# The first feed-forward of a two-block layer stack by seven block products

## The chip, the cores and the metric

The kernel runs on one core of one Trainium2 chip. The time is the device time of one execution in microseconds (us); the median of several executions is what a version is judged by. The engines are named as in the profile: PE is TensorE's matmul, PEld its weight load, DVE VectorE, ACT ScalarE, POOL GpSimd, SP SyncE, which issues most of the loads.

## The reference, cut to the stage that changes

Two blocks work on 1024 tokens (1040 rows with 16 meta rows in front) of width 1024. The first block ends in a gated feed-forward of width 2816, which is 22 tiles of 128:

```python
D_FF, CONV_WIDTH, N_META = 2816, 3, 16

def causal_dwconv(x, w, b):
    L = x.shape[1]
    xp = jnp.pad(x, ((0, 0), (CONV_WIDTH - 1, 0), (0, 0)))
    y = b
    for j in range(CONV_WIDTH):
        y = y + xp[:, j:j + L] * w[j]
    return y

...
        h = h + rmsnorm(z @ w_out[l], mix_norm_post[l])
        u = rmsnorm(h, ffn_norm_pre[l])
        gt = causal_dwconv(u @ ffn_w_gate[l], ffn_conv_w[l], ffn_conv_b[l])
        y = (jax.nn.gelu(gt, approximate=True) * (u @ ffn_w_up[l])) @ ffn_w_down[l]
        h = h + rmsnorm(y, ffn_norm_post[l])
    return h[:, N_META:]
```

The second block follows: attention and an mLSTM side by side, a cross-attention over 256 memory rows, and 32 experts. It starts with a norm of h and a projection.

## The kernel before, in words

Everything is kept feature by token: 128 features on the partitions, tokens along the free axis. Fp32 accuracy comes from splitting both operands of every matmul into a high part (an fp32r copy, made by ACT) and a low part (the rest, a subtraction on DVE). `mm3` (lines 417 to 424) then does three matmuls for each k tile: high by high, high by low, low by high. SBUF is an arena of 48 slots of 1040 fp32 columns (`Slots`), taken and given back by hand. `Stream` (line 194) loads weight blocks of 128x1024 in the fixed order that `all_blocks` lists, and splits them ahead of their use (lines 228 and 229).

PSUM has eight banks in three rings: four `mm`, two `lv`, two `ms`. Work that should run later is put off with `K.after(us, fn)`; `K.tick` counts matmul columns as a clock and calls what is due (lines 394 to 402). Step-wise background work hangs in `K.bg` and moves one step for each tile (`K.step`). After the program is written, a scheduler sets the order in which each engine's instructions stand; each engine then takes them strictly in that order.

`ffn` (line 1099) does the feed-forward of the first block. `gu` (line 1124) makes the gate of an f tile in three chunks of 342 tokens (the first three f tiles together in chunks of 256 or 258, as their input comes out of the preceding stage in these chunks), then `gate_conv` the convolution on DVE and the gelu on ACT, then the up product in two chunks of 512, whose result `up_out` multiplies with the gelu and splits into m's parts. `down` (line 1138) takes two f tiles of m and adds their part of all eight output tiles to y in SBUF: 16 results of 512 tokens, each 6 matmuls and one DVE addition (line 1149). So for each two f tiles PE does 144 matmuls of 342 columns and 192 of 512.

The last `down` goes token chunk by token chunk (256), and `last` hangs a `post_pre` (line 554) behind each of the four chunks. `post_pre` is the seam between two stages: `first` (norm of the result, residual, squares) and, later, `second` (the next stage's norm and the split of its input by `norm_apply`, line 579). DVE, ACT and POOL share this work. While it runs, `mem_kv` (line 1587) gives PE the keys and values of the memory rows, and `block2_mix` (line 1206) starts with `tm`, eight token tiles of 24 matmuls of 392 columns that read the normed tokens.

Of the kernel before, what the change touches and what calls it, by code (L numbers as in the profile page):

```python
# [20 lines left out]
D = 1024  # L21
KT = 8
# [171 lines left out]
class Stream:  # L194


    def __init__(self, k, blocks, raw=3, ahead=2):
        self.k, self.blocks = k, blocks
        self.raw_n, self.ahead = raw, ahead
        self.loaded = self.split = self.taken = 0  # L200
        self.raw, self.parts = {}, {}
        self.rings, self.own = {}, ()

# [16 lines left out]
    def pump(self):  # L220
        k = self.k
        while self.split < min(self.taken + self.ahead, len(self.blocks)):
# [13 lines left out]
    def _load(self):  # L236
        k = self.k
        while self.loaded < len(self.blocks) and len(self.raw) < self.raw_n:
# [64 lines left out]
class Kern:  # L303
# [250 lines left out]
    def post_pre(self, s, n, yv, hv, post, pre, store, uh, ul, t1=2.0, t2=18.0, done=None):  # L554
# [14 lines left out]
        def second():  # L569
# [5 lines left out]
            self.norm_apply(yv, hv, r, pre, uh, ul, n)  # L575
# [26 lines left out]
def block1(K):  # L602
# [458 lines left out]
    def ev_y(f, ps, s, n):  # L1061
        nc.scalar.activation(K.f(y + f, s, s + n), ps[:, :n], AF.Copy)
        K.sum_sq(s, n, ps[:, :n], f == 0)
        if f < 7:
# [5 lines left out]
                   done=lambda: c < 2 and hload(c + 2))  # L1070
# [18 lines left out]
MEMF = 18  # L1089
LAG, HS, GS = 3, 4, 3  # L1090
DEC = {256: ((0, 4),)}
# [6 lines left out]

def ffn(K, u2h, u2l, h1d, rest, y):
    nc, sl, st = K.nc, K.sl, K.st  # L1100
    act = K.act([u2h + k for k in range(8)], [u2l + k for k in range(8)])
    ms = {}

    def gate_conv(f, g):
# [10 lines left out]
    def up_out(f, c, ps, s, n):  # L1115
        x = s - 16
        nc.vector.tensor_mul(K.f(c, x, x + n), ps[:, :n], K.f(c, x, x + n))
        if f not in ms:
            ms[f] = sl.take()
        nc.scalar.activation(K.r(ms[f], x, x + n), K.f(c, x, x + n), AF.Copy)  # L1120
        nc.vector.tensor_sub(K.r(c, x, x + n), K.f(c, x, x + n), K.rf(ms[f], x, x + n))

    def gu(fs):
# [5 lines left out]
        K.dense((len(fs),), 8, Q1026 if fs[0] == 0 else C1026, act, ev_g)  # L1129
        if fs[0] == 0:  # L1130
            rest()
        cs = [gate_conv(f, g) for f, g in zip(fs, gs)]
        K.dense((len(fs),), 8, C1024, act, lambda j, ps, s, n: up_out(fs[j], cs[j], ps, s, n))
        for f, c in zip(fs, cs):
            ms[f] = (ms[f], c)

    def down(g, last=None):
        ks = [2 * g, 2 * g + 1]
        ws = [st.next() for _ in ks]
        order = [(o, c) for c in QX for o in range(8)] if last else [(o, c) for o in range(8) for c in CX]  # L1140
        for o, (s, n) in order:
            ps = K.bank("dn")[:, :n]
            wh = [K.r(w[0], o * 128, o * 128 + 128) for w in ws]
            wl = [K.r(w[1], o * 128, o * 128 + 128) for w in ws]
            K.mm3(ps, wh, wl, [K.r(ms[k][0], s, s + n) for k in ks], [K.r(ms[k][1], s, s + n) for k in ks])
            if g == 0:
                nc.scalar.activation(K.f(y + o, s, s + n), ps, AF.Copy)
            else:
                nc.vector.tensor_add(K.f(y + o, s, s + n), ps, K.f(y + o, s, s + n))  # L1149
            if last:  # L1150
                last(o, s, n)
            K.tick(3 * len(ks), n)
        for w in ws:
            st.done(w)
        for k in ks:
            sl.give(ms[k][0])
            sl.give(ms[k][1])

    st.ahead = 2
    gu([0, 1, 2])  # L1160
    for f in range(3, NF + 1):
        if f == MEMF:
            mt = sl.take(2)
            mem = mem_norm(K, mt)
            sl.give(mt, 2)
        if f % 2 == 1:
            down((f - 3) // 2)
        if f < NF:
            gu([f])

    uh, ul = u2h, u2l
    st.ahead = 1
    xd = K.dram.tile([128, 8, T2], F32, name="xd")
    K.sums(QX)
    hcs = [sl.take(2) for _ in range(2)]
# [5 lines left out]
    def last(o, s, n):  # L1181
        K.sum_sq(s, n, K.f(y + o, s, s + n), o == 0)
        if o < 7:
            return
        c = QX.index((s, n))
        K.post_pre(s, n, K.f3(y, 8, s, n), K.flat3(hcs[c % 2], KT, n), "ffn_post", "norm_mix",
                   xd[:, :, s:s + n], K.r3(uh, 8, s, n), K.r3(ul, 8, s, n),
                   t1=2.5 + 8.0 * c, t2=20.0 + 8.0 * c, done=lambda: c < 2 and hload(c + 2))

    hload(0)  # L1190
    hload(1)
    down(NF // 2 - 1, last)

    def rest():
# [5 lines left out]
        st.ahead = 2  # L1200

# [4 lines left out]
def block2_mix(K, uh, ul, xd, rest):  # L1206
# [7 lines left out]
    def tm(nb, kb, n, evac):  # L1214

        ws = [st.next() for _ in range(nb)]
        for t in range(8):
# [29 lines left out]
    tm(4, 2, 392, ev_c)  # L1247
    rest()
# [232 lines left out]
    for h in range(4):  # L1481
# [4 lines left out]
        if h == 3:  # L1486

            atl = sl.take(4)
            av = K.f3(atl, 4, 0, T2)
            nc.sync.dma_start(av, attd.rearrange("j p t -> p j t"))  # L1490
            for k in range(4):
                nc.vector.scalar_tensor_tensor(av[:, k], av[:, k], K.p("att_out", k), K.f(asq, 0, T2), op0=OP.mult, op1=OP.mult)
# [94 lines left out]
def mem_kv(K, mh, ml):  # L1587
# [3 lines left out]
    kx, vx = sl.take(), sl.take()  # L1591
# [591 lines left out]
def all_blocks(A):  # L2183
    b = [A["w1"][j] for j in range(A["w1"].shape[0])]
    G, U, W = A["w_gate"], A["w_up"], A["w_down"]
    b += [G[0], G[1], G[2], U[0], U[1], U[2]]
    for f in range(3, NF + 1):
        if f % 2 == 1:
            b += [W[f - 3], W[f - 2]]
        if f < NF:  # L2190
            b += [G[f], U[f]]
    b += [W[NF - 2], W[NF - 1]]
# [10 lines left out]
    return b  # L2203


def program(ctx, tc, A, out, dbg=None):
    K = Kern(ctx, tc, A, out, dbg)
    K.load_consts()
    K.st = Stream(K, all_blocks(A))
# [43 lines left out]
```

## Time and profile before

| | us |
|---|---|
| median of 3 runs (2885.87 to 2891.96) | 2886.0 |
| the profiled execution | 2889.72 |
| its span, first to last instruction | 2887.9 |
| PE busy | 2739.0 |
| DVE busy | 1735.2 |
| ACT busy | 1357.0 |
| POOL busy | 451.3 |
| first feed-forward, first gate result to last down result | 765.5 to 1519.4 |

A busy PE is not a PE at its peak, since matmuls overlap in the records: the time of a matmul in a stream is read from the distance between results, not from its own duration. Where times of a row are spaced more closely than its duration, the spacing is what a further instruction costs.

### The profile page before, as it was taken

Reading aid. Unit: us, or ns where it says so; the run is one execution under the profiler, and the core shown is the slowest. Engines: PE = TensorE matmul, PEld = TensorE weight load, DVE = VectorE, ACT = ScalarE, POOL = GpSimd, SP = SyncE. Lnnn points to the kernel's source line nnn. Section 1 sums busy time; section 2 is a strip of 40 time slices with the busy share of each in tenths; the row PEclk is TensorE's granted clock in tenths of the full one; section 3 lists DMA queues with packets and bytes.
Section 4 is the critical chain, followed back from the end, with each engine's and each line's share of the span. In section 5 each row is a group of like instructions: output and inputs, shape, how many; then the busy total and the mean of one; then the engine's idle time right before and its main releaser. Section 6 shows DMA issues by size and latency. Waiting matters only on the chain. (4 is left out here: it accounts for less than half of the span.)

```text
span 2887.9 us, 40429 instructions
## 1 busy us (share of the span) xinstructions
PE 2739.0 (95%) x15834; PEld 2346.6 (81%) x15834; DVE 1735.2 (60%) x2658; ACT 1357.0 (47%) x2267; POOL 451.3 (16%) x452
## 2 busy tenths in 40 slices
PE   7999999999899999999998999999998999899995
PEld 7999999999888888888887877778897666666663
DVE  7755621144734444445459264785746899999985
ACT  5546432234431221223135265553544788687775
POOL 4322120034500000000035000011401111111110
PEclk8999999999999999999999999999999999999997
DMA  4000113333511111111115111022116999999996
GB/s 156 23 30 23 37 66 110 115 122 86 117 59 52 44 50 46 52 44 39 64 59 161 66 45 52 15 98 86 34 69 224 333 358 364 327 356 369 365 361 225
DMA packets 118944, 382.74 MB, mean 133 GB/s; under 512 B 13100, under 2 KB 29612, under 8 KB 117984
## 3 DMA queue, kind: packets, MB, share of 16 engines
q1 hardware_dynamic: 88080, 319.71, 30.5%
q0 software_dynamic: 11040, 38.56, 5.3%
q10 hardware_dynamic: 19632, 21.87, 2.7%
q8 instruction: 125, 2.05, 0.3%
q14 instruction: 67, 0.55, 0.1%
HBM read 338.12 MB, written 46.16 MB: 133 GB/s over the span
## 5 line engine op out<-in xcount | busy, mean ns | idle before, releaser
L422 PE MATMUL ps_mm<-r,r 128*128 128x342 f32 (+6 forms) x2928 | 967.3, 330 | 4.2 <-DVE f L1037 2.3
L424 PE MATMUL ps_mm<-r,r 128*128 128x342 f32 (+6 forms) x2928 | 957.1, 327 | 1.9 <-DVE r L229 1.9
L423 PE MATMUL ps_mm<-r,r 128*128 128x342 f32 (+6 forms) x2928 | 954.1, 326 | 0.0
L229 DVE TENSOR_TENSOR r<-f,r 128x1024 fp32r<-128x1024 f32 (+1 forms) x549 | 659.7, 1224 | 443.3 <-ACT r L228 270.2
L228 ACT ACTIVATE r<-f 128x1024 fp32r<-128x1024 f32 (+1 forms) x549 | 569.7, 1056 | 477.8 <-PE ps_lv L423 156.0
L422 PEld LDWEIGHTS ps_mm<-r,r 128*128 128x128 f32 x2928 | 554.0, 189 | 40.6 <-issue 7.9
L424 PEld LDWEIGHTS ps_mm<-r,r 128*128 128x128 f32 x2928 | 553.5, 189 | 30.6 <-DVE r L229 3.0
L423 PEld LDWEIGHTS ps_mm<-r,r 128*128 128x128 f32 x2928 | 554.4, 189 | 28.9 <-DVE r L1500 0.3
L2055 PE MATMUL ps_mm<-r,r 128*96 128x512 f32 x512 | 207.2, 405 | 31.2 <-DVE r L229 31.2
L2054 PE MATMUL ps_mm<-r,r 128*96 128x512 f32 x512 | 204.8, 400 | 0.6 <-ACT r L228 0.6
L2056 PE MATMUL ps_mm<-r,r 128*96 128x512 f32 x512 | 202.3, 395 | 0.0
L1149 DVE TENSOR_TENSOR f<-ps_lv,f 128x512 f32<-128x512 f32 (+1 forms) x176 | 112.4, 642 | 103.9 <-PE ps_lv L424 103.6
L422 PE MATMUL ps_lv<-r,r 128*128 128x512 f32 (+1 forms) x384 | 146.7, 382 | 7.1 <-DVE f L1149 7.1
L423 PE MATMUL ps_lv<-r,r 128*128 128x512 f32 (+1 forms) x384 | 145.6, 379 | 0.0
L424 PE MATMUL ps_lv<-r,r 128*128 128x512 f32 (+1 forms) x384 | 144.9, 377 | 0.0
L2055 PEld LDWEIGHTS ps_mm<-r,r 128*96 128x96 f32 x512 | 83.1, 162 | 70.6 <-DVE r L229 41.5
L694 ACT ACTIVATE f<-ps_mm 128x342 f32<-128x342 f32 (+2 forms) x99 | 44.8, 454 | 162.9 <-PE ps_mm L424 162.7
L2054 PEld LDWEIGHTS ps_mm<-r,r 128*96 128x96 f32 x512 | 83.1, 162 | 39.5 <-ACT r L228 7.6
L2030 POOL DMA_INDIRECT f<-xnd,lix x32 | 51.6, 1612 | 368.6 <-PE ps_lv L2056 303.2
L2056 PEld LDWEIGHTS ps_mm<-r,r 128*96 128x96 f32 x512 | 83.0, 162 | 31.1
L2054 PE MATMUL ps_lv<-r,r 128*96 128x512 f32 x256 | 102.2, 399 | 0.6 <-ACT r L2084 0.6
L2055 PE MATMUL ps_lv<-r,r 128*96 128x512 f32 x256 | 101.7, 397 | 0.0
(466 smaller groups left out, 3934.2 us busy)
## 6 DMA issues: line engine op xcount, KB each, us to landing
f<-in_e_gate_dram SPq DMA_DIRECT2D x128, 512.0 KB, 9.8
f<-in_e_down_dram SPq DMA_DIRECT2D x128, 512.0 KB, 9.9
f<-in_e_up_dram SPq DMA_DIRECT2D x128, 512.0 KB, 8.5
f<-in_w_dram SPq DMA_DIRECT2D x52, 512.0 KB, 4.0
f<-in_w_gate_dram SPq DMA_DIRECT2D x22, 512.0 KB, 3.6
f<-in_w_up_dram SPq DMA_DIRECT2D x22, 512.0 KB, 3.2
f<-in_w_down_dram SPq DMA_DIRECT2D x22, 512.0 KB, 3.3
gates<-f ACTq DMA_DIRECT2D x16, 513.0 KB, 6.1
```

Source lines behind the costliest of these rows:

```text
L228: k.nc.scalar.activation(k.r(h, 0, n), k.f(r, 0, n), AF.Copy)
L229: k.nc.vector.tensor_sub(k.r(l, 0, n), k.f(r, 0, n), k.rf(h, 0, n))
L422: mm(ps, wh[k], ah[k], start=start and k == 0, stop=False)
L423: mm(ps, wh[k], al[k], start=False, stop=False)
L424: mm(ps, wl[k], ah[k], start=False, stop=stop and k == n - 1)
L694: nc.scalar.activation(K.f(slot, s, s + n), ps[:, :n], AF.Copy)
L1149: nc.vector.tensor_add(K.f(y + o, s, s + n), ps, K.f(y + o, s, s + n))
L2030: nc.gpsimd.indirect_dma_start(out=K.f(g, 0, D)[:EB], out_offset=None, in_=R["xnd"][:, :], in_offset=IndirectOffsetOnAxis(ap=ix[:, 0:1], a ...
L2054: mm(ps, xh, wh, start=first, stop=False)
L2055: mm(ps, xh, wl, start=False, stop=False)
L2056: mm(ps, xl, wh, start=False, stop=last)
```

## The change

The 22 f tiles are 11 pairs. Two pairs (f 0 to 3) are still done as before, without `down`. For the other nine pairs, gate and up are each a product of a 2x2 block matrix of weights (two f tiles by two halves of k) with a 2x2 block matrix of inputs (two halves of k by two halves of tokens, 514 each with two columns of overlap). It is done as seven products of blocks in place of eight: the class `Seven` makes four sums of weight blocks and the splits, `u_sums` and `u_parts` make the four sums of input blocks once, and `seven` does the seven products, each of 12 matmuls of 258 or 256 columns, in two chunks, with five additions on DVE behind them. Gate and up of a pair are called a pass each.

`down` is done at the end for all 22 f tiles: seven products, named 11, s1, s2, s3, s4, 12 and 22 by the weight block or sum that they use, of 11 steps each (one for each pair). A step is 12 matmuls of 512 columns into four banks. `keep` forms three sums of m's quarters and stores four quarters and three sums unsplit to DRAM (`mo`); a step loads one of them (256 KB) and a piece of the weights (256 or 512 KB), and `split` makes the parts. `result` adds the products into the quarters of y. The `post_pre` of tokens 512 to 1023 (chunks 2 and 3) is due during 12 and 22, that of chunks 0 and 1 behind 22. The norm of the memory rows moves from the middle of the feed-forward to behind s4. `tm` starts with token tiles 4 to 7, and finishes the put-off work before tile 0. At the seam ahead of the feed-forward, `first` is due at 4.5 in place of 2.0, and `norm_apply` leaves POOL out there (`n_pool=0`), as the input sums need y complete. Behind it the attention's output is loaded and split slot by slot.

```diff
+class Seven:
...
+        V.tensor_sub(s3, a11, a21)
+        V.tensor_add(s1, a21, a22)
+        yield
+        V.tensor_sub(s2, s1, a11)
+        V.tensor_sub(s4, a12, s2)
+        yield
+        high(ha, a)
+        yield
+        high(hb, b, 512, 528)
+        low(ha, a)
...
+HC = ((0, 258), (258, 256))
+WAIT = 5
...
+    def keep(j, cs, t):
...
+        V.tensor_sub(t1, m12, m11)
+        V.tensor_sub(m12, m22, m12)
+        V.tensor_sub(t2, m22, t1)
+        V.tensor_sub(t4, t2, m21)
+
+        def store():
+            for src, o, n in ((cs[0], 0, 2), (cs[1], 2, 2), (t[0], 4, 2), (t[1], 6, 1)):
+                nc.scalar.dma_start(mo[j, :, o:o + n], K.f(src, 0, 512 * n).rearrange("p (o n) -> p o n", o=n))
...
+        K.after(KEEP, store)
...
+    def seven(w, c0, n, at, first):
+
+        r12, r21, r22 = at
+        A_, D_, F_, E_, G_ = K.bank(), K.bank("lv"), K.bank(), K.bank("ms"), K.bank("lv")
+        product(A_, n, w.side("11"), "11", c0, True, True)
+        nc.scalar.activation(r12, A_[:, :n], AF.Copy)
+        product(D_, n, w.side("s3"), "t3", c0, True, True)
+        product(E_, n, w.side("s1"), "t1", c0, True, True)
+        nc.scalar.activation(r22, E_[:, :n], AF.Copy)
+        product(F_, n, w.side("22"), "t4", c0, True, True)
+        product(A_, n, w.side("12"), "21", c0, False, True)
+        first(A_)
+        product(G_, n, w.side("s2"), "t2", c0, True, True)
+        V.tensor_add(r12, G_[:, :n], r12)
+        V.tensor_add(r21, D_[:, :n], r12)
+        product(E_, n, w.side("s4"), "22", c0, False, True)
+        V.tensor_add(r22, r22, r21)
+        V.tensor_sub(r21, r21, F_[:, :n])
+        V.tensor_add(r12, E_[:, :n], r12)
...
+    def pair(j, wg):
...
+        wu = Seven(K, A["w_up"][fs[0]], A["w_up"][fs[1]])
+        group(wg, wu, gate)
+        wg.give()
+        cs = [gate_conv(f, g) for f, g in zip(fs, gs)]
...
+            V.tensor_mul(cc, r21[:, d:n], cc)
+            V.tensor_mul(ce, r22, ce)
+            V.tensor_mul(cb, r12, cb)
...
+        group(wu, wg, up)
...
+        keep(j, cs, t)
...
+    order = (("11", "11"), ("s1", "t1"), ("s2", "t2"), ("s3", "t3"), ("s4", "22"), ("12", "21"), ("22", "t4"))
...
+    gu([0, 1], mid0)
+    gu([2, 3], mid1)
+    K.drain()
...
+    for _ in u_parts("t1", [(u2h + k, HT[1]) for k in range(4)], q11, y, HT[0]):
+        pass
+    for _ in u_parts("t2", [(u2l + k, HT[1]) for k in range(4)], q22, y + 4, HT[1]):
+        pass
...
+        elif w == "s4":
+            squares(1, y12, False)
+            post((2, 3), 8.0, 22.0, 9.0)
...
+            mem.extend(mem_norm(K))
...
+        elif w == "22":
+            squares(0, y21, False)
+            post((0, 1), 6.0, 20.0, 7.0)
+
+    tags = {"11": "mm mm mm mm", "s1": "lv lv ms ms", "s2": "mm mm mm mm", "s3": "lv lv ms ms", "s4": "mm mm mm mm",
+            "12": "lv lv mm mm", "22": "mm mm lv lv"}
+    for i, (w, m, j) in enumerate(steps):
+        while len(loads) < min(i + LOADS - (w in ("12", "22")), len(steps)):
+            load()
+        while len(sides) < min(i + SIDES, len(steps)):
+            split()
+        if j == 0:
+            banks = [K.bank(t) for t in tags[w].split()]
+        a, b = sides[i]
+        mh, ml = K.r(b, 512, 1024), K.r(b, 0, 512)
+        for o in range(4):
+            wh, wl = K.r(a, 512 + o * 128, 640 + o * 128), K.r(a, o * 128, o * 128 + 128)
+            mm = nc.tensor.matmul
+            mm(banks[o], wh, mh, start=j == 0, stop=False)
+            mm(banks[o], wh, ml, start=False, stop=False)
+            mm(banks[o], wl, mh, start=False, stop=j == NP - 1)
...
-    tm(4, 2, 392, ev_c)
-    rest()
+    tm(4, 2, 392, ev_c, rest)
```

The order on DVE in the feed-forward before, one f tile (L229 is the low part of a weight block, L1108 and L1110 the convolution, L1117 and L1121 the product with the gelu and its split, L1149 the 16 additions into y):

```order
L229 TENSOR_TENSOR r_1_3351<-f_1_148,r_1_2061 128x1024
L1108 TENSOR_SCALAR f_1_433<-f_1_379,prm 128x1024
L1110 SCALAR_TENSOR_TENSOR f_1_433<-f_1_379,prm,f_1_433 128x1024 x2
L1117 TENSOR_TENSOR f_1_433<-ps_mm,f_1_433 128x512
L1121 TENSOR_TENSOR r_1_3343<-f_1_433,r_1_1603 128x512
L1117 TENSOR_TENSOR f_1_433<-ps_mm,f_1_433 128x512
L229 TENSOR_TENSOR r_1_193<-f_1_136,r_1_191 128x1024
L1121 TENSOR_TENSOR r_1_3343<-f_1_433,r_1_1603 128x512
L1149 TENSOR_TENSOR f_8_5488<-ps_lv,f_8_5488 128x512 x16
```

And now on DVE in the first chunk of a pair's up pass (L1187 ends the convolution of the two gates, L1140 to L1144 are the sums of the next pair's gate weights, L1138 a low part, L1287 to L1292 the additions behind the products, L1321 to L1324 the products with the gelu):

```order
L1187 SCALAR_TENSOR_TENSOR f_1_160<-f_1_352,prm,f_1_160 128x1024
L1321 TENSOR_TENSOR f_1_74<-ps_mm,f_1_74 128x254
L1140 TENSOR_TENSOR f_1_143<-f_1_120,f_1_136 128x512
L1143 TENSOR_TENSOR f_1_137<-f_1_137,f_1_120 128x512
L1287 TENSOR_TENSOR f_1_142<-ps_lv,f_1_142 128x258
L1144 TENSOR_TENSOR f_1_143<-f_1_120,f_1_137 128x512
L1288 TENSOR_TENSOR f_1_142<-ps_lv,f_1_142 128x258
L1138 TENSOR_TENSOR r_1_343<-f_1_120,r_1_199 128x1024
L1290 TENSOR_TENSOR f_1_148<-f_1_148,f_1_142 128x258
L1292 TENSOR_TENSOR f_1_142<-ps_ms,f_1_142 128x258
L1291 TENSOR_TENSOR f_1_142<-f_1_142,ps_mm 128x258
```

The additions behind the products now stand behind the two convolutions and between the sums and splits of the next weights.

DVE at the end of the down products, from the second norm of chunk 2 on (L576 and L1927 are reciprocals of norms, L593 to L598 `norm_apply`, L1376 the split of a step, L1469 the four additions that free the banks of product 12):

```order
L576 RECIPROCAL f_1_74<-f_1_74 128x256
L1376 TENSOR_TENSOR r_1_348<-f_1_154,r_1_348 128x512
L593 SCALAR_TENSOR_TENSOR f_8_5488<-f_2_12089,prm,f_1_74 128x256 x5
L1376 TENSOR_TENSOR r_1_2061<-f_1_124,r_1_2061 128x512
L595 TENSOR_TENSOR r_8_164<-f_8_5488,r_8_163 128x2x256 x2
L595 TENSOR_TENSOR r_8_164<-f_8_5488,r_8_163 128x256
L598 SCALAR_TENSOR_TENSOR r_8_164<-f_8_5488,prm,r_8_163 128x256 x3
L1927 RECIPROCAL f_1_149<-f_1_149 128x256
L1469 TENSOR_TENSOR f_8_5488<-ps_lv,f_8_5488 128x512
L593 SCALAR_TENSOR_TENSOR f_2_5456<-f_2_5456,prm,f_1_149 128x256 x5
```

The remaining three L1469 stand behind the memory rows' `norm_apply`; before the change, no norm stood between the additions of `down` and PE's next matmul into their banks except in the last `down`.

## Rows read from the trace of the kernel before

**Rows 1.** The page: busy time, share of the span and instructions by engine.

```profile
PE 2739.0 (95%) x15834; PEld 2346.6 (81%) x15834; DVE 1735.2 (60%) x2658; ACT 1357.0 (47%) x2267; POOL 451.3 (16%) x452
```

**Rows 2.** Stretches: length, busy PE, PEld, DVE, ACT, POOL, granted clock, DMA share, GB/s.

```profile
1002.04:1069.46 67.42, 67.42 (x337) 58.78 (x336) 30.00 (x38) 13.32 (x18) 0.00 (x0) 1.00 0.14 48
660.00:680.00 20.00, 20.00 (x170) 20.00 (x169) 2.45 (x2) 7.69 (x17) 4.10 (x5) 1.00 0.37 132
1484.00:1602.00 118.00, 99.60 (x560) 90.29 (x560) 100.46 (x165) 64.25 (x130) 61.95 (x75) 0.91 0.40 131
2500.00:2600.00 100.00, 95.93 (x481) 67.48 (x479) 92.12 (x116) 79.76 (x96) 14.76 (x10) 1.00 1.02 360
```

**Rows 3.** Timeline of ACT, copies behind 24 matmuls: start, duration, then what.

```profile
1014.87 0.46 ACT L1127 ACTIVATE f<-ps_mm 128x342 f32<-128x342 f32 x1 [2.44 <-PE ps_mm L424]
1018.65 0.46 ACT L1127 ACTIVATE f<-ps_mm 128x342 f32<-128x342 f32 x1 [3.32 <-PE ps_mm L424]
...
660.93 0.38 ACT L1062 ACTIVATE f<-ps_mm 128x256 f32<-128x256 f32 x1 [2.17 <-PE ps_mm L424]
663.77 0.39 ACT L1062 ACTIVATE f<-ps_mm 128x256 f32<-128x256 f32 x1 [2.18 <-PE ps_mm L424]
...
680.93 0.39 ACT L1062 ACTIVATE f<-ps_mm 128x258 f32<-128x258 f32 x1 [2.20 <-PE ps_mm L424]
683.83 0.39 ACT L1062 ACTIVATE f<-ps_mm 128x258 f32<-128x258 f32 x1 [2.23 <-PE ps_mm L424]
```

**Rows 4.** Timeline of DVE: results of `down`, then dense runs (xN in one row).

```profile
1045.59 0.69 DVE L1149 TENSOR_TENSOR f<-ps_lv,f 128x512 f32<-128x512 f32 x1 [0.72 <-PE ps_lv L424]
1046.99 0.69 DVE L1149 TENSOR_TENSOR f<-ps_lv,f 128x512 f32<-128x512 f32 x1 [0.71 <-PE ps_lv L424]
...
1036.13 1.28 DVE L1149 TENSOR_TENSOR f<-ps_lv,f 128x512 f32<-128x512 f32 x2
...
1504.35 0.74 DVE L1149 TENSOR_TENSOR f<-ps_lv,f 128x256 f32<-128x256 f32 x2
...
1024.50 0.81 DVE L1108 TENSOR_SCALAR f<-f,prm 128x1024 f32<-128x1024 f32 x1
1025.34 2.60 DVE L1110 SCALAR_TENSOR_TENSOR f<-f,prm,f 128x1024 f32<-128x1024 f32 x2
```

**Rows 5.** Groups of instructions: the weight loads of line 422, busy us, mean ns.

```profile
L422 PEld LDWEIGHTS ps_mm<-r,r 128*128 128x128 f32 x2928 | 554.0, 189 | 40.6 <-issue 7.9
```

**Rows 6.** DMA: issues with us to landing; queues with packets, MB, share.

```profile
f<-in_w_down_dram SPq DMA_DIRECT2D x22, 512.0 KB, 3.3
...
q1 hardware_dynamic: 88080, 319.71, 30.5%
...
q10 hardware_dynamic: 19632, 21.87, 2.7%
```

**Rows 7.** PE's waits from 640 to 765 (us, times, longest), and DVE at chunk 3.

```profile
PE ps_ms L546 <- POOL f L540: 10.5, 4, 7.4
...
783.93 3.25 DVE L591 SCALAR_TENSOR_TENSOR f<-f,prm,f 128x256 f32<-128x256 f32 x5
```

**Rows 8.** Timeline of DVE: parts of `post_pre` at the end of the feed-forward.

```profile
1494.62 1.74 DVE L548 RECIPROCAL f<-f 128x256 f32<-128x256 f32 x1
...
1496.56 1.75 DVE L562 SCALAR_TENSOR_TENSOR f<-f,prm,f 128x256 f32<-128x256 f32 x2
...
1533.86 3.49 DVE L591 SCALAR_TENSOR_TENSOR f<-f,prm,f 128x256 f32<-128x256 f32 x5
...
1540.00 2.35 DVE L229 TENSOR_TENSOR r<-f,r 128x1024 fp32r<-128x1024 f32 x2
```

**Rows 9.** Groups by shape: one operation of DVE beside busy POOL, and without.

```profile
L562 DVE SCALAR_TENSOR_TENSOR f<-f,prm,f 128x256 f32<-128x256 f32 x56 | 44.1, 826 | 0.0
...
L596 DVE SCALAR_TENSOR_TENSOR r<-f,prm,r 128x256 fp32r<-128x256 f32 x36 | 15.7, 475 | 0.1
```

More of the change, by code (lines that the diff above doesn't have):

```diff
@@ L1 @@
 import math
+from functools import partial
 from contextlib import ExitStack
@@ L221, in pump @@
         k = self.k
-        while self.split < min(self.taken + self.ahead, len(self.blocks)):
+        while self.split < min(self.taken + self.ahead, self.limit):
             self._load()
@@ L1069, in ev_y @@
                    h1d[:, :, s - T0:s - T0 + n], K.r3(u2h, 8, s, n), K.r3(u2l, 8, s, n),
-                   done=lambda: c < 2 and hload(c + 2))
+                   t1=4.5, done=lambda: c < 2 and hload(c + 2), n_pool=0)
     hload(0)
@@ L1159, in ffn, with up_out, act0 @@
[L1159 to L1169, printed above, removed]
+        def up_out(j, ps, s, n):
+            c = K.f(cs[j], s - 16, s - 16 + n)
+            V.tensor_mul(c, ps[:, :n], c)
+        def act0(s, n):
+            if s == Q1026[-1][0]:
+                rest()
+            return act(s, n)
@@ new lines, in early, with product @@
+    def early():
+        for _ in u_sums():
+            yield
+        for n, q, lo, l0 in (("t3", q12, HT[1], y), ("t4", q21, HT[0], y + 4)):
+            t = [sl.take() for _ in range(2)]
+            new.extend(t)
+            yield from u_parts(n, [(t[k // 2], k % 2 * HN) for k in range(4)], q, l0, lo)
+    def product(ps, n, w, b, c0, start, stop):
+        wh, wl = w
+        bh, bl = ops[b]
+        K.mm3(ps[:, :n], wh, wl, [K.r(x, o + c0, o + c0 + n) for x, o in bh], [K.r(x, o + c0, o + c0 + n) for x, o in bl],
+              start, stop, skip_group_check=True)
+        K.step()
+        K.tick(12, n)
@@ new lines, in begin, with mid0, mid1 @@
+    def begin():
+        for _ in range(4):
+            load()
+        for _ in range(8):
+            yield
+        for _ in range(2):
+            split()
+            yield
+    new = []
+    st.limit = st.blocks_first
+    st.ahead = st.raw_n = 1
+    K.steps = 1
+    def mid0():
+        zeros()
+        K.bg.append(early())
+    def mid1():
+        w.append(Seven(K, A["w_gate"][4], A["w_gate"][5]))
+        K.bg.append(w[0].prep())
+    w = []
+    gu([0, 1], mid0)
+    gu([2, 3], mid1)
@@ L1171, in ffn @@
     uh, ul = u2h, u2l
-    st.ahead = 1
     xd = K.dram.tile([128, 8, T2], F32, name="xd")
+    pairs = [sl.take(2) for _ in range(3)]
+    S += [x + o for x in pairs for o in range(2)]
     K.sums(QX)
-    hcs = [sl.take(2) for _ in range(2)]
+    hcs = []
+    mem = []
     def hload(c):
@@ L1191, in ffn, with quarter, squares @@
-    hload(1)
-    down(NF // 2 - 1, last)
+    def quarter(i, j):
+        return [K.f(y + 4 * i + o, 512 * j, 512 * j + 512) for o in range(4)]
+    y11, y12, y21, y22 = quarter(0, 0), quarter(0, 1), quarter(1, 0), quarter(1, 1)
+    def squares(j, ys, first):
+        acc = K.f(K.sq[0], 512 * j, 512 * j + 512)
+        for o, v in enumerate(ys):
+            if first and o == 0:
+                nc.scalar.activation(acc, v, AF.Square)
+            else:
+                x = K.f(K.sq[1], o % 2 * 512, o % 2 * 512 + 512)
+                nc.scalar.activation(x, v, AF.Square)
+                nc.gpsimd.tensor_add(acc, acc, x)
@@ L2184, in all_blocks @@
     b = [A["w1"][j] for j in range(A["w1"].shape[0])]
[L2185 to L2192, printed above, removed]
+    G, U = A["w_gate"], A["w_up"]
+    b += [G[0], G[1], U[0], U[1], G[2], G[3], U[2], U[3]]
+    first = len(b)
     for n in ("w2_ck", "w2_cv", "w2_c", "KQ", "w2_tm", "QK", "w2_o", "w2_cq", "w2_co"):
```

328 lines of the change are left out of this document (250 added, 78 removed).

## The prediction

> **What bounds the kernel now.** I read the page's busy times first. PE is busy 95% of the span and DVE 60% [rows 1]. Matmuls overlap in the records, so that share does not yet say that PE sets the pace; the stretches of time do. One period of the feed-forward (two f tiles) lasts 67.42 us with PE busy throughout, while DVE is busy 30.00 and POOL never [rows 2]. A period has 144 matmuls of 342 columns and 192 of 512. The distances between results price them: 3.78 us from copy to copy for 24 matmuls of 342, so 0.1575 us each [rows 3], and 1.40 us from addition to addition for 6 of 512, so 0.2337 each [rows 4]. 144 x 0.1575 + 192 x 0.2337 = 67.6, the period. So in this stage a column less is time less, as long as DVE keeps up. At the end of the feed-forward it is the other way round: from 1484 to 1602, 118.0 us, DVE is busy 100.46 and PE waits [rows 2].
>
> **The passes.** The results of 24 matmuls stand 2.84 us apart at 256 columns and 2.90 at 258 [rows 3]: 0.1183 and 0.1208 us each. Gate and up of a pair cost 144 x 0.1575 + 96 x 0.2337 = 45.1 us now. Seven products of 12 matmuls in two chunks, twice, are 2 x (84 x 0.1208 + 84 x 0.1183) = 40.2. Nine pairs gain 9 x 4.95 = **44.6 us**.
>
> **Down.** Ten of the eleven `down` rounds cost 96 x 0.2337 = 22.4 each, the last one, in chunks of 256, 192 x 0.1183 = 22.7; together 247.1. Afterwards there are 7 x 11 steps of 12 matmuls of 512, 924 x 0.2337 = 215.9, a step being 2.80. Gain **31.2 us**. So PE's own work shrinks by 75.8.
>
> The short matmuls hang on the weight loads, of which a row says 189 ns each [rows 5]. That mean is no price: in the stage with 256 and 258 columns PEld is busy all 20.00 us and results still come every 0.118 us per matmul [rows 2, 3]; the loads overlap. The Trainium skill, "TensorE: Matmul & The Clock Gate", section "Back-to-back issue gap", speaks against short matmuls: it says that weight load and matmul together set the spacing and that the column formula undercounts at small widths. By that formula the two gains would be an estimated 71 us rather than 76; the rows at 256 show about 9 ns above the formula, and it is the rows that I use.
>
> **What DVE must do inside a pass.** For a pair: the sums of weights (2 x 5 operations of 512 at 0.64) and low parts (2 x 3 of 1024 at 1.17) [rows 4, 8], 13.4; five additions of about 258 in each of four chunks, 20 x 0.37 [rows 4], 7.4; eight products with the gelu, 3.0; two convolutions, 2 x (0.81 + 2.60) [rows 4], 6.8; `keep`, 4 x 0.64, 2.6. Together 33.2 of 40.2 us, 83%, against 45% before. So the cover holds, but it is thin: the order puts both convolutions and sums of the next weights ahead of the additions of the up pass. The up pass holds some 20.2 us of DVE work in 20.1, and only the gate pass behind it, with about 13, has room. Product 9 of the next chunk waits for a `lv` bank that such an addition frees, by my count with 0.5 to 0.8 us to spare. I take **+4 us** (0.5 for a pair), between 0 and 27 (3 for a pair, the length of the convolution's two long operations that can stand in front).
>
> **The start.** Now PE waits 10.5 us behind the norms at the seam ahead of the feed-forward, 7.4 in one piece, and chunk 3's apply on DVE ends at 789.9 after the 3.25 us at 783.93 and what follows it [rows 7]. While that goes on, PE has the gate tiles of the first chunks, 24 matmuls or some 2.87 us for a tile and chunk; two tiles in place of three cover 6 x 2.87 = 17.2 us in place of 25.8, while `n_pool=0` gives DVE three more products for each chunk. The earlier due time gives back perhaps 4. I take **+5** (0 to 12). The input sums t1 and t2 are made behind the last up of f 2 and 3, eight sums and splits of DVE, partly uncovered: **+3** (0 to 6).
>
> **Transfers.** `keep` stores 7 x 256 KB a pair, and down loads them again with weights. A 512 KB weight load lands after 3.3 us [rows 6]. The share of queue time per packet (30.5% of 16 engines' span over 88080 packets of 3.6 KB; 2.7% over 19632 of 1.1 KB) gives about 160 and 64 ns for a packet [rows 6], so about 97 ns for 2 KB. A step with 256 such packets needs 1.6 us of the 16 engines, one of s1 or s3 with 384 needs 2.3, of 2.80. The queue has moved 360 GB/s in another stage [rows 2], and down wants 187, in s1 and s3 280. The loads are issued some five steps ahead on SP. I take **+2** (0 to 8). Nothing in the trace reads back from DRAM what was just written, so the upper end is a rival below.
>
> **The end of the feed-forward.** From the end of s4 to the end of `tm` PE has 61.7 (22 steps of 12 and 22) + 22.7 (`mem_kv`, 192 matmuls of 256) + 34.3 (`tm`, 192 of 392, at 0.179 by interpolation) = 118.7 us of work. Against that DVE has a list. Up to the split that the fourth step of 22 needs: 21 splits x 0.64, eight bank additions x 0.64, an allowance of 2.3 for the reductions of the squares, five reciprocals x 1.74 [rows 8], two `first` x 7.8 (from 1496.56 to the next work at 1504.35) [rows 8, 4], three applies x 6.1 (1533.86 to 1540.00) [rows 8]: some 63.5 us, against 14 steps x 2.80 = 39.3 of PE. The order shows why it hurts: the four additions that free the banks of product 12 stand behind chunk 2's apply, and three of them behind the memory rows' apply. PE loses about 25 there and about 11 more in `tm`, whose fourth weight split stands behind chunk 0's apply. That is 36. Before, the same work (last `down`, `mem_kv`, `tm`) is 22.7 + 22.7 + 34.3 = 79.7 of 118.0, so 38.3 are lost now at a granted clock of 0.91 [rows 2]. The wait stays and changes its place: **0**, between -20 (the additions overtake, or the norms finish under 12 and 22) and +15 (the two halves each wait).
>
> This list is priced from rows beside busy POOL. There, one operation of 256 takes 826 ns, and a nearly equal one where POOL rests 475 [rows 9]: a factor of 1.74. The Trainium skill, "SBUF — State Buffer", section "Who interferes with whom", says that DVE with two SBUF inputs contends with POOL reading SBUF; those rows agree. I price the end at the slow durations, the passes at the fast ones, since POOL has nothing in them.
>
> The slot-wise load of the attention's output and the new order of `tm`'s tiles I take at **0** (3 either way): the slots come free in the order in which the tiles want them.
>
> **The sum.** -44.6 - 31.2 + 4 + 5 + 3 + 2 + 0 + 0 = -61.8. The profiled execution took 2889.7, 3.7 above the median of the runs; it becomes 2827.9, and against the median 2886.0 the forecast is **2824 us**.
>
> **The rivals.** *The end is covered better* (14%): if DVE is done with chunks 2 and 3 before product 22 begins, its 20 us come off: about 2804. For it: these norms are due early in 12. Against it: the order of the additions.
>
> *The passes are partly paced by DVE* (13%): each pair loses 3 to 3.5 us more than I took, nine pairs about 30: 2854. For it: 83% and the long operations in front. Against it: the work that slips has the gate pass to catch up in.
>
> *The load path bounds down* (6%): if the loads of a step follow each other at 3.3 us per 512 KB [rows 6], 77 x 3.3 = 254 against 216, +38: about 2862. Against it: q1 moved 360 GB/s in other stages, so loads overlap.
>
> *DVE becomes the bound of the passes altogether, slower than before* (4%). From 40.2 us of DVE a pair on, every microsecond counts nine times; the gain of 62 is used up at 40.2 + 62/9 = 47.1 us, a factor of 1.42 on my 33.2. A factor of 1.6, between 1 and the 1.74 of rows 9, makes 53 a pair, 9 x 13 = +115: about 2939. Against it: POOL is idle in these passes, and the 0.37 and 0.64 are of dense runs.
>
> *The weight loads bound the passes* (1%): 336 x 0.189 = 63.5 us a pair, 9 x 23.3 = +210 on the forecast: about 3034. The row of 256-column results contradicts it.
>
> That the change does not do what it says is left out: the order shows the products, widths and steps as described.
>
> **The numbers.** The forecast has 62%, its own range 2800 to 2848 from the ends above. The range runs from 2792 (the better end with a little more) to 2862 (slower passes or loads) and leaves out the two slower rivals, a part of the load path and the far low end. A measurement of this kernel can tell about 0.2%, 5.8 us, from no change. Faster: the first three cases and most of the load path, 93%; same 2%; slower 5%.
>
> **What would show it.** Right: PE 100% busy in the passes, a pair's gate and up every 40 to 41 us with DVE near 80%; steps of 2.8 us in 11 to s4; some 36 us of idle PE in 12, 22, `mem_kv` and `tm`, its waits in 22 at `lv` banks behind the four additions; 11 to 15 us at the start. Wrong: pairs of 43 us and more with PE waiting for additions at `lv`; steps of 3.3 with PE or DVE waiting for a DMA; an end that loses under 20 or over 50.

## The result and the profile after

The changed kernel takes 2840.6 us (median of 4 executions, 2836.2 to 2843.3), the kernel before 2889.0 (4 executions). The ratio is 0.983, 95% interval 0.9817 to 0.9843: 48 us faster. The forecast was 2824 us, 62 faster, with a range of 2792 to 2862. The profiled execution spans 2841.0 us in place of 2887.9, 46.9 less; the stages below are told in this execution's times. It took 2842.8 us by the device, near the upper end of the four. Their times go with PE's mean granted clock: 2836.2 us at 0.974, 2843.3 at 0.969.

The first row of the page, to be held against [rows 1]: PE is busy 59.8 us less, DVE 170.8 us more.

```profile
PE 2679.2 (94%) x16446; PEld 2322.7 (82%) x16446; DVE 1906.0 (67%) x3039; ACT 1427.9 (50%) x2408; POOL 434.9 (15%) x426
```

Stretches of the changed kernel (length, busy PE, PEld, DVE, ACT, POOL, granted clock, DMA share, GB/s): the start of the feed-forward, two pairs of passes, the down products 11 to s4, three pieces of products 12 and 22, the memory's products with `tm`, and the gates with the mLSTM.

```profile
751.00:790.50 39.50, 33.16 (x218) 30.98 (x217) 33.05 (x46) 15.94 (x34) 11.11 (x13) 0.87 0.38 67
1039.64:1121.06 81.42, 81.20 (x674) 80.37 (x673) 64.48 (x109) 26.28 (x41) 0.00 (x0) 1.00 0.29 98
1224.20:1377.00 152.80, 152.80 (x663) 124.08 (x662) 115.29 (x182) 72.59 (x124) 6.78 (x6) 1.00 0.78 262
1377.00:1410.00 33.00, 33.00 (x145) 26.89 (x144) 31.89 (x41) 19.79 (x38) 14.74 (x15) 1.00 0.57 188
1410.00:1450.00 40.00, 23.19 (x62) 15.78 (x61) 39.96 (x61) 19.56 (x40) 19.00 (x20) 0.72 0.55 164
1450.00:1470.00 20.00, 20.00 (x88) 16.28 (x87) 8.79 (x12) 6.52 (x9) 1.10 (x1) 0.97 0.31 106
1470.00:1538.00 68.00, 62.67 (x353) 59.38 (x353) 49.66 (x78) 32.15 (x62) 24.77 (x27) 0.95 0.45 150
1720.30:1911.00 190.70, 172.15 (x857) 137.31 (x858) 127.88 (x256) 92.08 (x170) 12.05 (x9) 0.90 0.19 67
```

What the reader is to see: in the passes PE is busy throughout, a pair takes 81.42 / 2 = 40.7 us, and DVE 32.2 of it. In 11 to s4 a step takes 152.8 / 55 = 2.78 us and PE never waits. Between 1410 and 1450 it is DVE that is busy throughout, and PE works 23 of 40 us at a granted clock of 0.72. And in the last row, far behind the change, the clock is 0.90. The same piece of program before, from the last step of the attention to the last one of the mLSTM, and at its beginning a stretch around the gates' transposes:

```profile
1781.80:1959.00 177.20, 166.24 (x864) 132.07 (x865) 123.18 (x251) 91.48 (x167) 11.41 (x9) 0.95 0.19 70
1810.00:1826.00 16.00, 16.00 (x73) 11.79 (x74) 8.62 (x16) 9.58 (x13) 0.00 (x0) 1.00 0.00 0
```

It took 177.2 us and takes 190.7 now: 13.5 lost, in lines of code that the change did not touch; their buffers lie in other slots. By the end of `tm` the changed kernel is 1601.1 - 1538.1 = 63.0 us ahead, by the end of the attention 61.5, by the end of the mLSTM 48, at its end 46.9. So the forecast of 61.8 was met where the change ends, and 16 us were given back behind it in this execution.

PE's waits of the changed kernel, first from 1377 to 1470 and then from 1720 to 1911 (us in total, times, longest):

```profile
PE ps_mm L1510 <- DVE r L1376: 7.7, 3, 3.6
PE ps_lv L1509 <- DVE f L1469: 6.3, 2, 4.7
PE ps_ms L574 <- POOL f L568: 2.9, 2, 1.4
...
PE ps_ms L1760 <- ACT f L1723: 5.6, 2, 4.9
PE ps_mm L1558 <- DVE r L231: 5.1, 1, 5.1
PE ps_lv L1783 <- DVE f L1766: 4.8, 1, 4.8
PE ps_ms L1696 <- DVE f L1682: 3.0, 1, 3.0
```

The wait of L1696, the transposes of the mLSTM's gates, is new in this size (0.6 us before). DVE in front of it (start, duration, and in brackets its idle time and what ended it):

```profile
1718.89 0.73 DVE L1671 TENSOR_SCALAR f<-ps_ms,prm 4x512 f32<-4x512 f32 x1
1724.11 1.23 DVE L231 TENSOR_TENSOR r<-f,r 128x1024 fp32r<-128x1024 f32 x1 [4.49 <-DMA attd<-f]
1725.60 0.91 DVE L1677 MEMSET f<- 4x1024 f32 x1 [0.27 <-DVE r L231]
1726.57 0.07 DVE L1679 MEMSET f<- 4x8 f32 x1
1744.55 1.40 DVE L1671 TENSOR_SCALAR f<-ps_ms,prm 4x512 f32<-4x512 f32 x2 [17.91 <-PE ps_mm L1558]
1750.62 1.21 DVE L1676 SCALAR_TENSOR_TENSOR f<-f,f 4x1024 f32<-4x1024 f32 x1 [4.68 <-ACT f L1675]
...
1757.49 1.20 DVE L1682 TENSOR_TENSOR f<-f,f 4x1024 f32<-4x1024 f32 x1
```

DVE stands still for 17.9 us before it copies the second gate row out of PSUM, and what lets it go is a matmul of the attention's value product (L1558) that has nothing to do with the gates. In the program's order that row lies in slot 26, which held a weight block of that product. DVE also stood still here before the change, for 12.2 us behind the same product, but then the first scan was already done. Now the chain through ACT and two scans starts only there, and PE reaches its end 3.0 us too early. The clock of PE behind that wait, in pieces of 4 us:

```profile
1756.00:1760.00 4.00, 1.25 (x9) 1.23 (x10) 4.00 (x6) 1.68 (x2) 0.00 (x0) 0.79 0.00 0
1760.00:1764.00 4.00, 4.00 (x10) 3.13 (x10) 2.41 (x4) 3.27 (x3) 0.00 (x0) 0.50 0.00 0
1764.00:1768.00 4.00, 4.00 (x16) 1.63 (x15) 1.88 (x4) 2.55 (x5) 0.00 (x0) 0.86 0.00 0
1768.00:1772.00 4.00, 4.00 (x11) 3.04 (x11) 3.26 (x7) 0.78 (x3) 0.00 (x0) 0.57 0.02 4
```

It was 1.00 in the stretch 1810 to 1826 before.

### The profile page after: what moved, and what is told of

Read it like the earlier page. It is cut to its first block, busy times and chain, and to the rows that moved or that the text cites. A ratio compares the mean times of both kernels' runs of the same rounds, so it can differ in the third digit from the quotient of the medians.

```text
span 2841.0 us, 42887 instructions
## 1 busy us (share of the span) xinstructions
PE 2679.2 (94%) x16446; PEld 2322.7 (82%) x16446; DVE 1906.0 (67%) x3039; ACT 1427.9 (50%) x2408; POOL 434.9 (15%) x426
## 4 chain that ended last, share of the span: by engine, by line
PE 50%; DVE 9%; DMA 8%; ACT 4%; issue 3%; POOL 2%; SPq 0%; ACTq 0%; DVEq 0%; POOLq 0%
PE ps_mm L424 6%; PE ps_mm L426 6%; PE ps_mm L425 6%; DVE r L231 4%; DMA f<-in_e_down_dram 3%; DMA f<-in_e_gate_dram 2%; PE ps_mm L2406 2%; DMA f<-in_e_up_dram 1%; ACT r L230 1%; PE ps_mm L2407 1%; PE ps_mm L1510 1%; PE ps_mm L1511 1%; PE ps_mm L2405 1%; PE ps_mm L1509 1%; PE ps_mm L1557 1%
## 5 line engine op out<-in xcount | busy, mean ns | idle before, releaser
L424 PE MATMUL ps_mm<-r,r 128*128 128x256 f32 (+6 forms) x2632 | 842.0, 320 | 9.6 <-ACT r L594 4.1
L426 PE MATMUL ps_mm<-r,r 128*128 128x256 f32 (+6 forms) x2632 | 827.1, 315 | 0.5 <-DVE r L231 0.5
L425 PE MATMUL ps_mm<-r,r 128*128 128x256 f32 (+6 forms) x2632 | 826.8, 315 | 0.0
L231 DVE TENSOR_TENSOR r<-f,r 128x1024 fp32r<-128x1024 f32 x491 | 590.8, 1228 | 287.4 <-ACT r L230 144.6
L230 ACT ACTIVATE r<-f 128x1024 fp32r<-128x1024 f32 x491 | 507.8, 1055 | 208.0 <-PE ps_lv L2407 46.1
L424 PEld LDWEIGHTS ps_mm<-r,r 128*128 128x128 f32 x2632 | 501.7, 191 | 37.7 <-ACT f L1282 6.1
L425 PEld LDWEIGHTS ps_mm<-r,r 128*128 128x128 f32 x2632 | 501.8, 191 | 17.5 <-issue 1.0
L426 PEld LDWEIGHTS ps_mm<-r,r 128*128 128x128 f32 x2632 | 501.2, 190 | 16.2 <-DVE r L231 0.7
L1375 ACT ACTIVATE r<-f 128x512 fp32r<-128x512 f32 x154 | 91.0, 626 | 98.3 <-DMA f<-in_w_down_dram 27.2
L1376 DVE TENSOR_TENSOR r<-f,r 128x512 fp32r<-128x512 f32 x154 | 104.3, 714 | 40.1 <-ACT r L1375 38.8
L1135 ACT ACTIVATE r<-f 128x1024 fp32r<-128x1024 f32 (+1 forms) x72 | 66.6, 949 | 92.1 <-DMA f<-in_w_up_dram 51.0
L2405 PE MATMUL ps_lv<-r,r 128*96 128x512 f32 x256 | 101.9, 398 | 0.6 <-ACT r L2435 0.6
L2406 PE MATMUL ps_lv<-r,r 128*96 128x512 f32 x256 | 101.1, 395 | 0.0
L2407 PE MATMUL ps_lv<-r,r 128*96 128x512 f32 x256 | 101.0, 395 | 0.0
```

Source lines behind the costliest of these rows:

```text
L230: k.nc.scalar.activation(k.r(h, 0, n), k.f(r, 0, n), AF.Copy)
L231: k.nc.vector.tensor_sub(k.r(l, 0, n), k.f(r, 0, n), k.rf(h, 0, n))
L424: mm(ps, wh[k], ah[k], start=start and k == 0, stop=False)
L425: mm(ps, wh[k], al[k], start=False, stop=False)
L426: mm(ps, wl[k], ah[k], start=False, stop=stop and k == n - 1)
L1135: act(K.r(h, 0, m), K.f(x, o, o + m), AF.Copy)
```

## The experiments

Two theories of the 16 us behind `tm`: the **slot theory** (buffers that later stages draw from the pool were freed by other users than before), and its rival, that weights or attention stores come later. Two of the end of the feed-forward: the **list theory** of the prediction (DVE has more work than PE there, whatever its order), and the **order theory** (PE loses what one block of a norm delays the next split or bank). And the prediction's passes: how much cover DVE has left. All runs stand beside 2840.6 us.

**Gate rows in other slots** (e1_rows).

```diff
-    sl.give(ka)
-    sl.give(qa, 4)
...
-    rows = [sl.take() for _ in range(5)]
+    rows = [qa, qa + 1, qa + 2, qa + 3, ka]
```

> Only the place of five gate rows of the mLSTM is changed: they lie in the slots of the attention's queries and keys, not in slots that the last value product's weights held. Slot theory: the DVE evacuations at 1717 to 1744 us no longer wait for PE (17.9 us of idle DVE gone), the 2.99 us wait of the first 4x4 transposes goes and the low clock behind it too, so the stretch from the last attention step to the end of the transposes falls from 45 to 36-38 us, as before the change, and the run takes 2831 us (7 to 11 less than the changed kernel). Rival (the stretch is longer because weights or attention stores come later): nothing moves, within 2 us. Everything up to there stays within 1 us.

2831.9 us, ratio to the kernel before 0.9803 (0.9786 to 0.9819): 8.7 us better than the changed kernel. DVE of this kernel at the same place:

```profile
1716.58 1.39 DVE L1669 TENSOR_SCALAR f<-ps_ms,prm 4x512 f32<-4x512 f32 x2
1720.35 1.23 DVE L231 TENSOR_TENSOR r<-f,r 128x1024 fp32r<-128x1024 f32 x1 [2.38 <-DMA attd<-f]
1721.49 0.73 DVE L1669 TENSOR_SCALAR f<-ps_ms,prm 4x512 f32<-4x512 f32 x1
```

The 17.9 us are gone, the scans run under the value product, the transposes wait for nothing and end at 1741 in place of 1766, 23 us behind the attention's last step and not 36 to 38 as expected. Gates and mLSTM together:

```profile
1718.00:1900.50 182.50, 165.38 (x858) 132.50 (x859) 127.66 (x255) 89.89 (x169) 12.07 (x9) 0.94 0.20 73
```

182.5 in place of 190.7: the slot theory is right in direction, and by the medians the rows' place is worth 8.7 us here, and 6.4 on top of e5_c3b (e9_best below). How much of the 13.5 us it explains is less clear. Six other kernels here (e2_dve to e7_dve8) copy the second gate row as late as the changed kernel (22 to 26 us behind the attention's last step), and the same stretch, between the same two steps, takes 182.7 to 189.5 us in them. The shortest is e3_mem, with 18.3 us of idle DVE, the 3.0 us wait of the transposes and a mean clock of 0.94, as in e1_rows, where the changed kernel has 0.90. Without the late row it takes 182.5, 181.8 and 180.0 (e1_rows, e9_best, e10_c2), still more than 177.2. In e1_rows the transposes come 25 us earlier, but later waits in the mLSTM (for L1721 10.0 us in place of 5.6) take part of it back. What set those off was not tried, and the edit leaves other slots for later stages too.

**More work for DVE in the passes** (e2_dve, e7_dve8).

```diff
-        V.tensor_sub(s3, a11, a21)
-        V.tensor_add(s1, a21, a22)
+        for _ in range(4):
+            V.tensor_sub(s3, a11, a21)
+            V.tensor_add(s1, a21, a22)
```

(`range(8)` in e7_dve8.)

> Two of the five sums of a pair's weights are done four times over (same values), which adds 6 additions of 512 for each pass: 12 x 0.64 = 7.7 us of DVE a pair, 32.2 to 39.9 of 40.9. Theory of the prediction (DVE has the gate pass to catch up in, PE sets the pace): 0 to 1.5 us a pair, the nine pairs take 368 to 382 us in place of 368.6. Rival (DVE is on the path in the up pass already): each added microsecond counts, up to +7.7 a pair, the nine pairs take about 437 us and the run 2905.

> Two of the five sums of a pair's weights are done eight times over (same values): 28 x 0.64 = 17.9 us more of DVE a pair, 50.1 in all. The price of the prediction's slower rival: beyond 40 us DVE sets the pace, a pair takes 49 to 52 us, the nine passes 441 to 468 in place of 368.6, and the run 2915 to 2940. If DVE were not able to hold PE up (its work done in between), the nine would stay under 400.

e2_dve: 2840.2 us, ratio 0.9825 (0.9809 to 0.9841); the nine pairs take 376.0 us (854.6 to 1230.6), 0.8 a pair more. DVE is busy 38.1 us a pair in place of 32.0, so 6.1 more and not the 7.7 of the sum. e7_dve8: 2914.0, ratio 1.0088 (1.0068 to 1.0109); the nine take 446.5, 49.6 a pair, 8.7 more than the changed kernel's, with DVE busy 47.2 us a pair, 15.2 more. The same 100 us of both, e2_dve first:

```profile
1000.00:1100.00 100.00, 97.18 (x800) 95.83 (x800) 94.41 (x162) 32.93 (x50) 0.00 (x0) 1.00 0.24 81
```

```profile
1000.00:1100.00 100.00, 84.66 (x661) 83.41 (x661) 94.24 (x158) 23.76 (x38) 0.00 (x0) 0.93 0.23 80
```

DVE is busy 94% of these 100 us in both, so its share does not tell which engine sets the pace; PE's does. In e2_dve PE works 97 of 100 us, and its waits behind DVE's additions come to 7.3 us in all nine pairs. In e7_dve8 they come to 59.5 us, DVE sets the pace, and PE's clock falls too. So the cover had some 6 us a pair to spare. The slower rival came true where it was put: it gave 47.1 us of DVE a pair as the end of the gain, and with 47.2 the run is 25 us slower than the kernel before. The pair then takes 49.6 us, longer than DVE's own work. The 7.4 us that e2_dve loses in the passes do not show in its total (at the end of `tm` it is 7.9 behind, at its own end 0.7), since the same code behind `tm` took 7.2 us less in this execution; so the stage is read.

**The memory norm taken out of the end** (e3_mem): done behind the first pair, kept in DRAM, loaded at the end of s4.

```diff
     gu([0, 1], mid0)
+    mk = mem_norm(K)
...
-            mem.extend(mem_norm(K))
+            mem.extend([sl.take(2) for _ in range(2)])
+            for x, v in zip(mem, mk):
+                nc.gpsimd.dma_start(K.fl(x, 0, 2048, F32R), v)
...
```

> The norm of the memory rows is done behind the first pair, while DVE is some 65% busy, and kept in DRAM until the end of s4: 3.9 + 1.7 + 3.2 + 3.3 = 12 us less of DVE's work between 1377 and 1452 us. Theory (the list of DVE sets the end of products 12 and 22): the stretch from the end of s4 to the end of tm falls from 161 to 145-149 us. Rival (the order of the additions that free product 12's banks, not the length of the list, holds PE): only the waits behind the additions go, 161 to 153-157. Rival of no gain: the list moves other norms into the gap and tm waits instead, 159 or more. The start of the feed-forward grows by 0 to 2 us. The slots of later stages move too, so the time of the run may differ by a further 10 us either way behind tm.

2845.0 us, 0.9848 (0.9832 to 0.9865). From the end of s4 to the end of `tm` it takes 163.3 us, not less than 161.1. That is the number of the rival of no gain, but PE waits in 12 and 22 and not in `tm`. PE's waits in 12 and 22 of this kernel:

```profile
PE ps_mm L1513 <- DVE r L1376: 11.1, 1, 11.1
PE ps_lv L1512 <- DVE f L1470: 5.5, 1, 5.5
PE ps_mm L1512 <- DVE f L1468: 3.5, 1, 3.5
```

The next split now stands behind the whole apply of chunk 3, in which DVE itself stands still for 4.3 us until ACT has made the high part, and PE waits 11.1 us at once. A shorter list did not help in this order. But DVE's busy time in the stretch fell only from 130.3 to 125.8 us, not by the 12 of the expectation, and the order changed with it, so the list theory is not refuted. (The start lost a further 9.3 us there, to a weight split that came late.)

**The order on DVE at the end** (e4_late, e5_c3, e5_c3b): the memory's second half due later, then chunk 3's second norm as well.

```diff
-    K.after(26.0, second)
+    K.after(44.0, second)
```

```diff
-            post((2, 3), 8.0, 22.0, 9.0)
+            post((2, 3), 8.0, 22.0, 9.0, 42.0)
```

(The fifth number is the step of the second norms' due times, 30 in e5_c3 with the memory at 36, 42 in e5_c3b with the memory at 44.)

> The second half of the memory norm is due at 44 in place of 26 behind s4, so that the four additions that free product 12's banks need not stand behind its apply. Order theory: the two waits at these banks (1.6 + 4.7 us) and the low clock behind them go, the stretch from the end of s4 to the end of tm falls by 5 to 9 us. List theory: DVE's work is the same up to the memory's keys and values, so PE gets to wait elsewhere (at the splits of 22 or in the memory's products) and the stretch stays within 3 us of 161.

> On top of the late memory norm (here due at 36), the second norm of chunk 3 is due at 52 in place of 31 behind s4, so that on DVE six splits of product 22 stand ahead of the memory's apply and seven more ahead of chunk 3's. Order theory (PE loses what one apply delays the next split, not DVE's total work): the 8.0 us wait behind chunk 3's apply of the run with the late memory norm goes with the low clock behind it, the stretch from the end of s4 to the end of tm falls from 158 there to 145-151 us and the run to 2819-2825 us. List theory (DVE's work decides): the wait comes back in the memory's products or in tm, the stretch stays at 155-159.

> As e5_c3, but the memory's second half at 44 and chunk 3's second norm at 64, behind all of product 22: fifteen splits in a row on DVE. Order theory: no wait for splits in 22 any more, the end of the down products comes 85-88 us after that of s4 in the changed kernel's 94 and the late memory norm's 88, to 72-78; chunk 3's apply then falls into the memory's products with chunk 0's norms behind it, and tm gives back 5 to 10 us of it: stretch 145-153. List theory: 155-159 here too.

| | from the end of s4 to the end of `tm` | DVE busy in it | us |
|---|---|---|---|
| changed kernel | 161.1 | 130.3 | 2840.6 |
| e4_late | 156.5 | 133.9 | 2830.4 |
| e5_c3 | 153.5 | 132.5 | 2829.1 |
| e5_c3b | 150.8 | 134.9 | 2828.6 |

(The 158 of the expectations was read from 1.5 us earlier on.) Ratios to the kernel before: 0.9793 (0.9776 to 0.9809), 0.9793 (0.9777 to 0.9809), 0.9792 (0.9775 to 0.9808). PE's waits in 12 and 22 of e5_c3b:

```profile
PE ps_mm L1510 <- DVE r L1376: 9.5, 3, 8.0
PE ps_ms L548 <- POOL f L1446: 1.2, 1, 1.2
PE ps_mm L1509 <- ACT r L1375: 0.6, 1, 0.6
PE ps_lv L1509 <- DVE f L1469: 0.4, 1, 0.4
```

The order theory is right in direction: with no less work on DVE the stretch loses 10 us, and the end of the down products comes 77.6 us behind that of s4, not 92.5. Its sizes were missed in part. e4_late gained 4.6 us of the stretch where 5 to 9 were expected: the waits at the banks went, but one of 8.0 us at a split came. e5_c3's stretch lies between the two theories (145 to 151, or 155 to 159), and its time above the 2819 to 2825. In e5_c3b PE was to wait for no split in 22 and waits 9.5 us, 8.0 of them behind chunk 2's apply. The totals follow only in part. What lies behind `tm` takes 1302.9 us in the changed kernel and 1297.9, 1296.3 and 1299.3 in these three, with the same code; so e4_late owes some 5 of its 10 us to that. In e2_dve, e3_mem, e7_dve8 and e8_tm, with the same lines there, it takes 1291.5 to 1299.6, and the executions of the changed kernel alone lie 7 us apart. Differences of a few us between totals are not put down to the end here.

**`tm`'s order put back** (e8_tm).

```diff
-        for t in (4, 5, 6, 7, 0, 1, 2, 3) if half else range(8):
-            if t == 0 and half:
-                half()
+        for t in range(8):
...
-    tm(4, 2, 392, ev_c, rest)
+    rest()
+    tm(4, 2, 392, ev_c)
```

> The order of tm's token tiles is put back (0 to 7, all put-off work finished ahead of them). Cover theory: tm waits for chunk 0's apply, which ends on DVE at 1511 us, and not for chunk 2's, its start moves from 1494 to 1510-1514 and its end by 8 to 14 us, the run takes 2848-2856. Rival (tm is covered anyway, since DVE's list is the bound): its end stays within 3 us of 1538.

2846.3 us, 0.9853 (0.9836 to 0.9869). `tm` starts at 1509.9 and ends at 1549.0, 10.9 later (8.5 counted from the end of s4), within the 8 to 14 expected; the run is 1.7 us below the range that was expected. The new order, with the put-off work finished in the middle of `tm`, is worth 8 us of the end.

**Both repairs together** (e9_best, of e1_rows and e5_c3b), and with chunk 2's second norm later too (e10_c2: `post((2, 3), 8.0, 34.0, 9.0, 30.0)`, memory at 48).

> The gate rows' place of e1_rows and the late second norms of e5_c3b together. If the two losses are separate (one at the end of the feed-forward, one in the mLSTM), the gains add: 2840.6 - 8.7 - 12.0 = 2820, 2817 to 2823. If the second only moves a wait that the first one's gain depends on, no better than the better of the two, 2828.

> On top of e9_best, chunk 2's second norm is due at 34 in place of 22 behind s4 and the memory's at 48, so that product 12's bank additions and ten splits of 22 stand ahead of every apply. Order theory: the 8.0 us wait behind chunk 2's apply in e5_c3b goes too with its low clock, the end of the down products comes 66-71 us after the end of s4 in place of 77.6, the stretch to the end of tm falls by 2 to 8 us, run 2813-2820. List theory: what is put off now fills the memory's products and tm, the stretch stays within 3 us of e9_best's.

e9_best: 2822.2 us, 0.9768 (0.9755 to 0.9782); the gains add, 2 us short of their sum. e10_c2: 2821.5, 0.9767 (0.9753 to 0.9780). In e10_c2 the down products end 72.3 us behind s4 in place of 77.5, and the stretch to the end of `tm` is 152.5 in place of 152.2: what was put off now makes the memory's products and `tm` wait. Here the list theory's expectation came true (within 3 us of e9_best), and the run missed the 2813 to 2820 of the order theory: this change of order gave nothing more. DVE is busy 134.6 of 152.5 us, and PE has 118.7 of work; whether DVE's work alone is the floor was not shown, as the one run that took work away changed the order as well.

## Why the prediction held, and which step failed

- **The passes.** 368.6 us for nine pairs, 40.95 each, against 40.2 + 0.5 by the sum: right, some 3 us too little in all. In a gate pass 84 matmuls take 9.95 us at 256 columns, as [rows 3] give (9.94). In an up pass they take 10.29, and 10.37 at 258 columns: some 0.33 us more in each chunk, all at one place in the fourth product. There a weight load waits for ACT's copy of the third result (L1282), 6.1 us in all by the page:

```profile
L424 PEld LDWEIGHTS ps_mm<-r,r 128*128 128x128 f32 x2632 | 501.7, 191 | 37.7 <-ACT f L1282 6.1
```

In the up pass `w.room` puts that result into the unused half of the slot that holds the fourth product's weights, and in the program's order the first matmul of that product waits for the copy. So most of the added 0.75 us a pair is a wait that the sum did not have, at a slot again and not at a `lv` bank; the waits in PE's own rows come to 1.7 us. The Trainium skill, "TensorE: Matmul & The Clock Gate", section "Back-to-back issue gap", gives N / 2.4 + 2.5 ns as the isolated gap, an estimated 109 ns for 256 columns, and warns that this counts too little at small widths in a stream of weight loads and matmuls: 9.95 us / 84 = 118 ns agree with the warning.
- **DVE in the passes.** 32.2 us a pair against 33.2 by the sum, and the cover holds up to the 38.1 of e2_dve. Right; neither rival that put DVE on the path came true.
- **Down.** Steps of 2.78 us against 2.80; no wait at 262 GB/s, so the +2 for loads was 0. Nothing was lost by reading back from DRAM.
- **The start.** 39.5 us for 8 gate tiles and chunks and 8 further matmuls, 24.9 of work, so 14.6 lost in place of 12.8 (47.2 for 12 at 2.87): +1.8 where the sum had +5. The term for the first pair (+3) was 0, since passes begin without a wait.
- **The end of the feed-forward.** 161.1 - 118.7 = 42.4 us lost against the 36 of the list and 39 before (119.0 - 79.7): the size was nearly right (+3 for 0), the reason was half right. The order that the prediction named, norms ahead of the four additions and of splits, is what can be bought back (10 us); that a shorter list helps was not shown by e3_mem. And the sign of being right, some 36 us of idle PE, was not met: PE is idle 22 us, 17 of them in 12 and 22, where 31 are lost. The rest is a lower clock and small matmuls of the norms. Of the 17, only 6.3 are waits at the `lv` banks; 7.7 are waits for splits.
- **Up to the end of `tm`** the forecast of 61.8 was met by 63.0, in part by luck: +3 in the passes and +3 at the end stand against -3 at the start, -3 for the first pair and -2 for the loads.
- **The step that failed**: "The slot-wise load of the attention's output and the new order of `tm`'s tiles I take at 0 (3 either way): the slots come free in the order in which the tiles want them." It is the only term of the sum for what lies behind `tm`. Up to the end of the attention it was nearly so (1.5 us given back). But slots are drawn from one pool by the age of their last use, and the change shifts that age for all that follows: the gates' row fell on a weight slot that PE was still to read. Attention, gates, mLSTM and the rest give back 16.1 us in the profiled execution. The same lines give back 4.6 to 12.7 in the profiles of the seven runs that change nothing behind `tm`. The gates' row accounts for 6 to 9 us by the medians (e1_rows, e9_best). That other slots cause the rest was not shown; its cause stays open. The term should have been some +10, 5 to 16 by these profiles, and a sum by stages could not show it. The changed kernel's order could have: it names the slot of each row.

## What to carry to other kernels

A change that alters when buffers are given back changes every later allocation from the same pool: look in the new order for instructions whose output lies where an earlier instruction's operand still is, also in stages whose code is untouched. On an engine that takes its work strictly in order, ask of each long block what short instruction behind it another engine is waiting for; due times that put releases and splits ahead of whole norms gave 10 us here for no work saved. And read a gain by its stage as well as by the total: the same lines behind `tm` take 1291.5 to 1302.9 us in eight profiles.

## What was unexpected in the hardware

PE's clock can make short waits dear. Behind the 3.0 us wait of the transposes it was granted 0.50 of its speed for a full 4 us; between 1410 and 1450 waits of 16.8 us go with a mean of 0.72 on what was executed. The level of 0.50 is 1.2 of its 2.4 GHz. The second fall, to a mean of 0.57 from 1768 to 1772, had no such wait ahead of it: from 1765.1 to 1768.1 PE ran mostly transposes of 4x4 and matmuls of four rows (L1696, L1748, L1754). The price is not fixed: behind the same 3.0 us wait e3_mem has 0.69 and 0.88 in the first two pieces of 4 us and 1.00 in the next two. In e7_dve8 a PE that works 85 of 100 us, with waits of up to 7.0 us, has a mean clock of 0.93, and in e2_dve one that works 97 keeps 1.00.
